# One 64 KB-row tile in place of tiles seven and eight of a contrast kernel on one core

## The chip, the core and the metric

The kernel runs on one core of a Trainium2 chip. A core has engines that work side by side, each through its own list of instructions in order: TensorE (PE in the profile, its weight loads PEld), VectorE (DVE), ScalarE (ACT), GpSimd (POOL) and SyncE (SP). Sixteen DMA engines carry data between the chip's large memory (HBM) and the core's working memory of 128 partitions (SBUF). A DMA is issued by one of the engines' sequencers; here SP issues all loads and ACT all stores. The metric is device microseconds (us) of one execution, and less is better.

## The reference

```
batch, c, h, w = 16, 3, 512, 512
x = random float32 in [0, 1);  factor = 1.5

mean = np.mean(x, axis=(2, 3), keepdims=True)
return np.clip(mean + factor * (x - mean), 0, 1)
```

There are 48 images of 512x512 float32 numbers, 50.33 MB in all. Each image needs its own mean before any of its pixels can be written. With that mean, a pixel becomes 1.5 x + (1 - 1.5) mean, cut to the range 0 to 1. So all 50.33 MB go in, and 50.33 MB come out.

## The kernel before

**Tiles.** A tile is four images: 128 partitions of 8192 numbers (`ROW`), 32 KB in each partition and 4.19 MB in all. An image fills 32 partitions. There are 12 tiles, counted from 0, so the seventh and the eighth are t = 6 and t = 7. In HBM a tile is one contiguous block, partition after partition.

**The ring.** SBUF holds one array `ring` of six slots (`BUFS`), one tile each; tile t lies in slot t % 6. Everything is done in place: a tile is loaded into its slot, summed there, overwritten with its result there, and stored from there. Tile t + 6 can be loaded only when the store of tile t has landed. The tile framework adds those waits; SP stands at each load until the slot is free.

**What is done with a tile.** `add` (lines 87 to 100) sums the 8192 numbers of every partition on ACT (line 96, a copy onto itself with an accumulator); tile 0 alone has part of its row summed on DVE (line 91). A matmul with a constant 128x128 matrix `blockw` (line 100) then sums the 32 partitions of each image, scales by (1 - factor) / pixels, and gives every partition its shift in a column of the PSUM array `bias`. `blockw` is made once by POOL (lines 62 to 72). `clip` (lines 102 to 114) runs two passes on DVE: factor times x plus shift (line 104), then max with 0 and min with 1 (line 112). `store` (line 85) is a DMA issued by ACT.

**The order.** The order is written out by hand (`tc.manual_schedule()`, lines 116 to 135), and each engine follows it. SP issues loads 0, 1, then tiles 2 and 3 with one DMA, tiles 4 and 5 with one DMA, then one DMA for each of the tiles 6 to 11. Tile 0 is clipped and stored in three pieces of 1024, 2048 and 5120 columns. From then on the loop clips tile t, sums tile t + 1 and stores tile t; for t = 1 and 3 the store is issued ahead of the sum, for the others behind it. As ACT both sums and issues stores, a store waiting on ACT holds up the sum behind it, and the other way about.

**The queues.** The profile calls the queue of the loads q1 and that of the stores q10. Each of the 16 DMA engines serves eight partitions of every transfer. A DMA moves one contiguous run as one packet, so a load of one tile is eight packets of 32 KB on each of the engines, and a load of two tiles is sixteen of them, the two tiles' rows in turn.

Of the kernel before, what the change touches and what calls it, by code (L numbers as in the profile page):

```python
# [1 line left out]

# [4 lines left out]


P = 128  # L10
ROW = 8192
BUFS = 6
FIRST = (1024, 3072)


@with_exitstack
def kernel(
    ctx: ExitStack,
    tc: tile.TileContext,
    x: bass.AP,  # L20
    factor: float,
    out: bass.AP,
):

    nc = tc.nc
    f32 = mybir.dt.float32
    Alu = mybir.AluOpType
    Act = mybir.ActivationFunctionType  # L30

    B, C, H, W = x.shape
    n_img, n_pix = B * C, H * W
    ppi = n_pix // ROW
    per_tile = P // ppi
    n_tiles = n_img // per_tile
    assert ppi * ROW == n_pix and per_tile * n_tiles == n_img

    factor = float(factor)
    wconst = (1.0 - factor) / float(n_pix)  # L40

    x_f = x.rearrange("b c h w -> (b c h w)")
    out_f = out.rearrange("b c h w -> (b c h w)")

    def dram(ap, t, c0=0, c1=ROW, n=1):
        run = [[P * ROW, n]] if n > 1 else []
        return bass.AP(
            tensor=ap.tensor, offset=t * P * ROW + c0, ap=[[ROW, P], *run, [1, c1 - c0]]
        )

    consts = ctx.enter_context(tc.tile_pool(name="consts", bufs=1))
    xpool = ctx.enter_context(tc.tile_pool(name="xpool", bufs=1))
    small = ctx.enter_context(tc.tile_pool(name="small", bufs=1))
    psum = ctx.enter_context(tc.tile_pool(name="psum", bufs=1, space=bass.MemoryType.PSUM))


    sums = small.tile([P, 2 * n_tiles], f32, name="sums")
    bias = psum.tile([P, n_tiles], f32, name="bias")

    blockw = consts.tile([P, P], f32, name="blockw")  # L60
    blocks = blockw.rearrange("p (a b) -> p a b", b=ppi)
    nc.gpsimd.memset(blockw, wconst)  # L62
    for base, step in ((0, -ppi), (ppi - 1, ppi)):
        nc.gpsimd.affine_select(  # L64
            out=blocks,
            in_=blocks,
            compare_op=Alu.is_ge,
            fill=0.0,
            base=base,
            pattern=[[step, per_tile], [0, ppi]],  # L70
            channel_multiplier=1 if step < 0 else -1,
        )


    ring = xpool.tile([P, BUFS, ROW], f32, name="ring")

    def slots(t, n=1, c0=0, c1=ROW):
        k = t % BUFS
        return ring[:, k, c0:c1] if n == 1 else ring[:, k : k + n, :]

    def load(t, n=1):
        nc.sync.dma_start(out=slots(t, n), in_=dram(x_f, t, n=n))  # L82

    def store(t, c0=0, c1=ROW):
        nc.scalar.dma_start(out=dram(out_f, t, c0, c1), in_=slots(t, 1, c0, c1))  # L85

    def add(t, c0=0):
        own = sums[:, 2 * t : 2 * t + 2]
        parts = []
        if c0:  # L90
            nc.vector.tensor_reduce(  # L91
                out=own[:, 0:1], in_=slots(t, 1, 0, c0), axis=mybir.AxisListType.X, op=Alu.add
            )
            parts.append(own[:, 0:1])
        part = slots(t, 1, c0)
        nc.scalar.activation(out=part, in_=part, func=Act.Copy, accum_out=own[:, 1:2])  # L96
        parts.insert(0, own[:, 1:2])
        shift = bias[:, t : t + 1]
        for k, part in enumerate(parts):
            nc.tensor.matmul(shift, blockw, part, start=k == 0, stop=k == len(parts) - 1)  # L100

    def clip(t, c0=0, c1=ROW):
        part = slots(t, 1, c0, c1)
        nc.vector.tensor_scalar(  # L104
            out=part,
            in0=part,
            scalar1=factor,
            scalar2=bias[:, t : t + 1],
            op0=Alu.mult,
            op1=Alu.add,  # L110
        )
        nc.vector.tensor_scalar(  # L112
            out=part, in0=part, scalar1=0.0, scalar2=1.0, op0=Alu.max, op1=Alu.min
        )

    with tc.manual_schedule():
        load(0)
        load(1)
        load(2, 2)
        load(4, 2)  # L120
        add(0, 4352)
        for c0, c1 in zip((0, *FIRST), (*FIRST, ROW)):
            clip(0, c0, c1)
            store(0, c0, c1)
        add(1)
        for t in range(1, n_tiles):
            clip(t)
            if t in (1, 3):
                store(t)
            if t + 1 < n_tiles:  # L130
                add(t + 1)
            if t not in (1, 3):
                store(t)
            if t + BUFS - 1 < n_tiles:
                load(t + BUFS - 1)


# [1 line left out]
_INS = ['x', 'factor']  # L139
_OUTS = [((16, 3, 512, 512), 'float32')]  # L140

_NUMBERS = {'factor': 1.5}


# [26 lines left out]
```

## Time and profile before

| What | Before |
|---|---|
| time, median of three runs | 239.47 us (239.06 to 239.49) |
| time of the profiled execution | 238.72 us |
| span of the profiled execution, first to last instruction | 237.0 us |
| busy in the span: PE / DVE / ACT / POOL | 7.6 / 112.1 / 82.9 / 1.0 us |
| one 128x8192 pass: ACT sum, DVE line 104, DVE line 112 | 7.03, 4.49, 4.43 us |
| bytes moved | 100.66 MB, half in, half out |

The profile is of one execution. Its span runs from the first to the last instruction; the 1.72 us between the span and that execution's time lie outside it. An engine's busy time leaves out the time in which its sequencer waits or issues DMAs. The slices of the profile's second part are a fortieth of the span, 5.9 us each.

### The profile page before, as it was taken

Reading aid. Unit: us, or ns where it says so; the run is one execution under the profiler, and the core shown is the slowest. Engines: PE = TensorE matmul, PEld = TensorE weight load, DVE = VectorE, ACT = ScalarE, POOL = GpSimd, SP = SyncE. Lnnn points to the kernel's source line nnn. Section 1 sums busy time; section 2 is a strip of 40 time slices with the busy share of each in tenths; the row PEclk is TensorE's granted clock in tenths of the full one; section 3 lists DMA queues with packets and bytes.
Section 4 is the critical chain, followed back from the end, with each engine's and each line's share of the span. In section 5 each row is a group of like instructions: output and inputs, shape, how many; then the busy total and the mean of one; then the engine's idle time right before and its main releaser. Section 6 shows DMA issues by size and latency. Waiting matters only on the chain.

```text
span 237.0 us, 211 instructions
## 1 busy us (share of the span) xinstructions
PE 7.6 (3%) x26; PEld 6.5 (3%) x26; DVE 112.1 (47%) x29; ACT 82.9 (35%) x25; POOL 1.0 (0%) x7
## 2 busy tenths in 40 slices
PE   0000000000000000000000000000000000000000
PEld 0000000000000000000000000000000000000000
DVE  0078708609990059979209407704902920950000
ACT  2050190299100894650380091083056029000000
POOL 1000000000000000000000000000000000000000
DMA  7999998999999999999999999999999999999996
GB/s 265 442 442 442 398 459 383 441 428 435 465 426 404 409 442 442 442 442 442 442 426 431 404 420 442 442 442 442 442 442 426 415 398 442 442 442 442 442 442 265
DMA packets 3712, 100.66 MB, mean 425 GB/s; under 512 B 384, under 2 KB 384, under 8 KB 512
## 3 DMA queue, kind: packets, MB, share of 16 engines
q1 hardware_dynamic: 1696, 50.33, 49.6%
q10 hardware_dynamic: 2016, 50.33, 49.2%
HBM read 50.33 MB, written 50.33 MB: 425 GB/s over the span
## 4 chain that ended last, share of the span: by engine, by line
DMA 39%; DVE 25%; another core or an unknown queue 11%; ACT 9%; issue 3%; PE 1%; ACTq 1%; SPq 0%
DMA out_dram<-ring 20%; DMA ring<-in_x_dram 18%; DVE ring L104 11%; DVE ring L112 11%; ACT ring L96 9%; DVE sums L91 2%; PE bias L100 1%; ACTq L85 1%; SPq L82 0%
## 5 line engine op out<-in xcount | busy, mean ns | idle before, releaser
L96 ACT ACTIVATE ring<-ring 128x8192 f32<-128x8192 f32 (+1 forms) x12 | 80.7, 6724 | 117.3 <-DMA ring<-in_x_dram 95.3
L104 DVE TENSOR_SCALAR ring<-ring,bias 128x8192 f32<-128x8192 f32 (+3 forms) x14 | 54.3, 3880 | 84.9 <-PE bias L100 84.9
L112 DVE TENSOR_SCALAR ring<-ring 128x8192 f32<-128x8192 f32 (+3 forms) x14 | 53.4, 3817 | 0.5
L100 PE MATMUL bias<-sums,blockw 128*128 128x1 f32 x26 | 7.6, 361 | 194.0 <-ACT ring L96 193.5
L100 PEld LDWEIGHTS bias<-sums,blockw 128*128 128x128 f32 x26 | 6.5, 312 | 195.0 <-ACT ring L96 177.7
L91 DVE TENSOR_REDUCE sums<-ring 128x1 f32<-128x4352 f32 x1 | 4.7, 4685 | 13.1 <-DMA ring<-in_x_dram 13.1
L96 ACT ACTIVATION_READ_ACCUMULATOR ring<-ring 128x1 f32 x12 | 2.2, 186 | 0.0
L96 ACT ACT_TABLE_LOAD x1 | 1.3, 1283 | 0.8 <-PEq L152 0.8
L64 POOL TENSOR_SCALAR_AFFINE_SELECT blockw<-blockw 128x128 f32<-128x128 f32 x2 | 0.6, 311 | 0.1
L62 POOL MEMSET blockw<- 128x128 f32 x1 | 0.2, 204 | 0.3 <-POOLq L152 0.3
L152 POOL MEMSET const-uint8-127<- 128x1 uint8 x1 | 0.1, 103 | 0.0
L152 POOL MEMSET const-bfloat16-1.0<- 128x1 bf16 x1 | 0.1, 102 | 0.0
L152 POOL MEMSET const-float32-0.0<- 128x1 f32 x1 | 0.1, 98 | 0.3 <-issue 0.3
L152 POOL MEMSET const-float32-1.0<- 128x1 f32 x1 | 0.1, 98 | 0.0
## 6 DMA issues: line engine op xcount, KB each, us to landing
out_dram<-ring ACTq DMA_DIRECT2D x11, 4096.0 KB, 48.5
ring<-in_x_dram SPq DMA_DIRECT2D x8, 4096.0 KB, 31.4
ring<-in_x_dram SPq DMA_DIRECT2D x2, 8192.0 KB, 59.5
out_dram<-ring ACTq DMA_DIRECT2D x1, 2560.0 KB, 37.3
out_dram<-ring ACTq DMA_DIRECT2D x1, 1024.0 KB, 25.8
out_dram<-ring ACTq DMA_DIRECT2D x1, 512.0 KB, 16.1
```

Of the source, the lines that this page charges most:

```text
L62: nc.gpsimd.memset(blockw, wconst)
L64: nc.gpsimd.affine_select(out=blocks, in_=blocks, compare_op=Alu.is_ge, fill=0.0, base=base, pattern=[[step, per_tile], [0, ppi]], channel ...
L85: nc.scalar.dma_start(out=dram(out_f, t, c0, c1), in_=slots(t, 1, c0, c1))
L91: nc.vector.tensor_reduce(out=own[:, 0:1], in_=slots(t, 1, 0, c0), axis=mybir.AxisListType.X, op=Alu.add)
L96: nc.scalar.activation(out=part, in_=part, func=Act.Copy, accum_out=own[:, 1:2])
L100: nc.tensor.matmul(shift, blockw, part, start=k == 0, stop=k == len(parts) - 1)
L104: nc.vector.tensor_scalar(out=part, in0=part, scalar1=factor, scalar2=bias[:, t : t + 1], op0=Alu.mult, op1=Alu.add,)
L112: nc.vector.tensor_scalar(out=part, in0=part, scalar1=0.0, scalar2=1.0, op0=Alu.max, op1=Alu.min)
L152: nc = _bacc.Bacc("TRN2", target_bir_lowering=False, num_devices=1)
```

## The change

- The constant `PAIR = (6, 7)` names two tiles that are treated as one tile of 128 rows of 16384 numbers (64 KB). The pair holds the same eight images; now an image fills 16 of the 128 rows. Slots 0 and 1 of the ring lie side by side in a partition, so a row of the pair is contiguous in SBUF as well as in HBM.
- It is loaded by two DMAs as before, but each now brings half of the columns: a run of 32 KB out of every 64 KB of HBM, into slot 0 and then into slot 1.
- Both halves are summed on ACT one after the other. Their matmuls use a second constant matrix, `widew`, with blocks of 16 rows, and gather in one column of `bias`: the matmul of the first half opens the sum, that of the second half closes it. Both halves are clipped after that.
- It is stored by one DMA of 8.39 MB with rows of 64 KB, issued behind the stores of t = 8 and t = 9 (the ninth and tenth tile) and ahead of those of 10 and 11.
- From t = 8 on, each tile is summed, clipped and stored in turn, so the store is issued ahead of the next tile's sum.
- Tiles 2 and 3 are loaded with a DMA each.

```
+PAIR = (6, 7)
...
     def dram(ap, t, c0=0, c1=ROW, n=1):
+        if t in PAIR:
+            wide, half = 2 * ROW, t - PAIR[0]
+            return bass.AP(
+                tensor=ap.tensor,
+                offset=PAIR[0] * P * ROW + half * ROW,
+                ap=[[wide, P], [1, n * ROW]],
+            )
...
+    def block_weights(name, rows):
+        w = consts.tile([P, P], f32, name=name)
+        blocks = w.rearrange("p (a b) -> p a b", b=rows)
+        nc.gpsimd.memset(w, wconst)
+        for base, step in ((0, -rows), (rows - 1, rows)):
+            nc.gpsimd.affine_select(
...
+    blockw = block_weights("blockw", ppi)
+    widew = block_weights("widew", ppi // 2)
...
+    def store_pair():
+        nc.scalar.dma_start(out=dram(out_f, PAIR[0], n=2), in_=slots(PAIR[0], 2))
...
-        shift = bias[:, t : t + 1]
+        if t in PAIR:
+            shift, w, start, stop = PAIR[0], widew, t == PAIR[0], t == PAIR[1]
+        else:
+            shift, w, start, stop = t, blockw, True, True
+        shift = bias[:, shift : shift + 1]
         for k, part in enumerate(parts):
-            nc.tensor.matmul(shift, blockw, part, start=k == 0, stop=k == len(parts) - 1)
+            nc.tensor.matmul(
+                shift, w, part, start=start and k == 0, stop=stop and k == len(parts) - 1
+            )
...
         load(0)
         load(1)
-        load(2, 2)
+        load(2)
+        load(3)
         load(4, 2)
...
-        for t in range(1, n_tiles):
+        for t in range(1, BUFS):
             clip(t)
             if t in (1, 3):
                 store(t)
-            if t + 1 < n_tiles:
+            if t + 1 < BUFS:
                 add(t + 1)
             if t not in (1, 3):
                 store(t)
-            if t + BUFS - 1 < n_tiles:
-                load(t + BUFS - 1)
+            load(t + BUFS - 1)
+        load(2 * BUFS - 1)
+        add(PAIR[0])
+        add(PAIR[1])
+        for t in PAIR:
+            clip(t)
+        for t in (8, 9):
+            add(t)
+            clip(t)
+            store(t)
+        store_pair()
+        for t in (10, 11):
+            add(t)
+            clip(t)
+            store(t)
```

## The prediction

> **What bounds the kernel now.** I read the page's second and third part first (are the DMA engines ever idle?), then its table of DMA issues.
>
> ```profile
> DMA  7999998999999999999999999999999999999996
> GB/s 265 442 442 442 398 459 383 441 428 435 465 426 404 409 442 442 442 442 442 442 426 431 404 420 442 442 442 442 442 442 426 415 398 442 442 442 442 442 442 265
> ...
> q1 hardware_dynamic: 1696, 50.33, 49.6%
> q10 hardware_dynamic: 2016, 50.33, 49.2%
> ```
>
> The two queues together fill 49.6 + 49.2 = 98.8% of sixteen engines' span; only the first and the last slice are not full. VectorE at 47% and ScalarE at 35% are far from it. The second view is busy time by stretches; the last two columns of a row are the DMA share and GB/s.
>
> ```profile
> 3.00:20.00 17.00, 1.15 (x4) 1.00 (x4) 6.17 (x4) 3.50 (x2) 0.00 (x0) 1.00 1.00 430
> ...
> 116.42:135.77 19.35, 0.59 (x2) 0.50 (x2) 8.92 (x2) 7.12 (x2) 0.00 (x0) 1.00 1.00 434
> ...
> 193.87:235.80 41.93, 0.58 (x2) 0.50 (x2) 8.92 (x2) 7.12 (x2) 0.00 (x0) 1.00 0.98 425
> ```
>
> The first row has loads alone, the second loads and stores in equal parts, the third stores alone. The rate is the same in all three, so neither direction nor their mixture is the limit: the engines themselves are. The trace's records of single packets say the same: the median 32 KB packet takes 1.213 us, for load and store alike, and one of 20 KB 0.761, of 8 KB 0.309, of 4 KB 0.159.
>
> That gives a budget. 100.66 MB are 192 packets of 32 KB on each engine, 192 x 1.213 = 232.9 us. The first packet starts at 1.81 and the last ends at 235.83, so the engines have 234.0 us for it: 1.1 us is lost, 0.65 of it in the first packet of each engine (mean 1.87 us in place of 1.213), most of the rest in loads between 35 and 54 us, some of which take 1.31 to 1.52 us. The other 3.0 us of the span are the start (1.81) and the end behind the last packet (1.18).
>
> Third, the order of time around the change, in the timeline: start, length, engine.
>
> ```profile
> 103.35 0.34 ACTq L85 DMA_DIRECT2D out_dram<-ring  x1
> ...
> 116.42 7.03 ACT L96 ACTIVATE ring<-ring 128x8192 f32<-128x8192 f32 x1 [12.25 <-DMA ring<-in_x_dram]
> ...
> 135.77 7.03 ACT L96 ACTIVATE ring<-ring 128x8192 f32<-128x8192 f32 x1 [12.23 <-DMA ring<-in_x_dram]
> ...
> 155.14 7.03 ACT L96 ACTIVATE ring<-ring 128x8192 f32<-128x8192 f32 x1 [12.25 <-DMA ring<-in_x_dram]
> ```
>
> The first row issues the store of tile 5; the others sum tiles 7, 8 and 9, each as its load lands, and further down tile 10 follows at 174.50, tile 11 at 193.87. By the landings' semaphores the store of tile 5 lands at 162.32, those of 6 to 11 at 181.72, 197.48, 207.17, 216.86, 226.52 and 236.18. The last store is issued at 210.65 and waits until 226.5 for those ahead of it. So the end is the store queue's length, not any computation.
>
> **The change part by part.**
>
> *Does the store queue run dry?* This decides, because stores 6 and 7 leave the place behind store 5. Loads wait only for the landings of stores 0 to 5, which keep their order and their time, so loads 6 to 11 land as before (97.02, 116.39, 135.75, 155.12, 174.47, 193.84). ACT: store 5 at 103.35, sum of 6 from 103.7 to 110.8 (it was 97.05; load 7 lands later, so nobody waits), sum of 7 at 116.42, its matmul done at 124.2 (row: sum 7.03 + read 0.19 + matmul 0.6). DVE then runs four passes, 124.2 + 2 x (4.49 + 4.43) + gaps = 142.1. Sum of 8 at 135.77, shift at 143.5, clip to 152.5, store 8 issued at 152.5. Store 5 holds the queue until 162.3: 9.8 us to spare. Store 9: load 155.12, sum, matmul and clip take 16.7, issued at 171.9, against the end of store 8 at 181.7 (the time of the old store 6: both share with loads 10 and 11). The pair is issued at 172.3, against 197.5. Store 10 at 174.5 + 16.7 = 191.2, against 216.9. Store 11 at 210.6, against 226.5. Every store is in the queue 9.8 us or more before its turn. Cost 0.
>
> *Waits that ACT now takes.* Store 8 waits on ACT for its clip until 152.5, and behind it stands the sum of 9, whose data land at 155.12; store 10 waits until 191.2, and the sum of 11 behind it starts at 193.84. 2.6 us to spare in both; and if a sum came later, the 9.8 us and 15.9 us above would still cover it. Cost 0.
>
> *The store of 64 KB rows.* From the packets of 20 and 32 KB: (1.213 - 0.761) / 12288 bytes = 36.8 ps a byte, so 0.008 us of a packet doesn't grow with its size. Eight packets of 64 KB in place of sixteen of 32 KB save 8 x 0.008 = 0.06 us. No row shows a packet over 32 KB. Low end: -0.06. High end: the slowest store packet seen is 1.220, 0.007 over the median, on sixteen: +0.1. I take -0.06, the line through four sizes.
>
> *Loads of half rows.* The same 16 packets of 32 KB per engine, but the rows that an engine reads one after the other lie 64 KB apart, and its neighbours' twice as far away as before. Low end 0: in the trace the engines already work at starts that are multiples of 32 KB apart, at 1.213. High ends by slower rows: the mean load packet between 20 and 50 us, 1.2275, would cost 16 x 0.0145 = 0.23; the edge of the slow group, 1.312, 16 x 0.099 = 1.6; the slowest, 1.522, 4.9. I take 0, as the runs stay 32 KB long and a load of two tiles, whose successive packets lie 4.19 MB apart, already ran near the full rate (430 GB/s from 36 to 54 us).
> A rule speaks against it: the Trainium skill, "DMA: Bandwidth & Descriptors", section "Latency and other measured facts", says that rows in HBM a large power of two apart slow copies, from a pitch of 512 KiB at full rate (207 GB/s per direction) to 164 at 2 MiB. By its figures 64 KB would be free, and the sum would stay; if its slope began as low as here, it would be the second case below.
>
> *Loads 2 and 3 apart.* One more issue on SP, 0.43 us by its neighbours, at 2.1 us, when the queue has 9.7 us of work and more; the next load isn't needed before 45. Tile 2 lands at about 34 (half of the stretch 22.77 to 45.27) in place of 45. Nothing starts sooner: its sum stands on ACT behind store 1, which waits for a clip until 45.33. Ends: 0, and -0.31, if all that the 337 load packets between 20 and 50 us lose (337 x 0.0145 / 16) came from alternating rows; I take 0, since the slow ones stand where the small store pieces of tile 0 land (35, 48, 65 us), and those remain.
>
> *The rest.* POOL makes `widew`: 0.20 + 2 x 0.31 = 0.8 us behind 1.76; first needed at about 111. Matmuls are as many. Both cost 0 under the 100 us that cover them.
>
> Sum: -0.06. The profiled execution's span goes from 237.0 to 236.9, its time from 238.72 to 238.66. The median of the runs is 0.75 above the profiled one, so 239.47 - 0.06 = 239.4.
> By the skill's same page (section "Where 436 GB/s comes from") a core's DMA ports carry at most 435.2 GB/s; by that 100.66 MB need at least 231.3 us, so no packing could win more than 1.6 of the 232.9 us. The trace's 433 in steady stretches agrees with such a ceiling.
>
> **The rivals.**
>
> *Half-row loads are slow (slower).* Place: loads 6 and 7, 78 to 117 us. Price 1.6 at 1.312 us a packet: 241.0; it decides from 1.243 us a packet (16 x 0.030 = 0.48). For it: loads are the only packets that vary at all (1.31 to 1.52 around 35 to 54). Against it: 960 later ones average 1.2156, with every kind of address.
>
> *A wait on a store's issue (slower).* If an issue behind the pair waits for the pair's landing (the program has few DMA semaphores, and they are used again), the queue runs dry at 216.9: 1.01 from issue to first packet (0.80 to 1.81) and 0.4 of spread between the sixteen landings, 1.4 in all: 240.9. Against it: no store of before shows such a wait, and at the pair's issue only loads 10 and 11 and stores 8 and 9 are under way.
>
> *The queue runs dry at 162 (slower).* Late stores alone cost nothing at first: loads 10 and 11 then have 15.8 us of work left at the full rate (6.1 of load 10 and 9.7 of load 11) and take the engines meanwhile. So it decides from 9.8 + 15.8 = 25.6 us beyond the 152.5 worked out for store 8; past that each us costs one. At 26.6 us late, 240.4. Against it: the rows that it is worked out from are steady to 0.02 us.
>
> *Early loads lose less (faster).* Both gains in full, -0.06 - 0.31 = -0.37: 239.1. To pass 0.2% it would need all of the 0.45 us lost after the first packets and the 0.06 as well, 239.0.
>
> *The pair's store is cut to 32 KB packets.* Then nothing is saved: 239.5.
>
> **How the numbers follow.** I hold 0.2% (0.48 us) to be about what a measurement of this kernel tells from no change; the three runs spread 0.43. Forecast 239.4, with the uncut and the cut pair: 0.65. Slow half rows: 0.15. A wait on an issue: 0.05. A dry queue: 0.02. Faster: 0.13, which also holds what the profiled execution may not show, since the runs are 0.75 above it. Slower by over 0.2% is 0.15 + 0.05 + 0.02 = 0.22. The likeliest case alone has 239.0 to 239.9. The range for 8 in 10 goes down to 238.9, past the faster case of 239.0, and up to 241.0, the slow half rows at 1.312; what is over that (packets slower still, two waits) I give 1 in 10.
>
> **What would show it.** Right: the DMA share by stretches stays 1.00 at 433 GB/s from 97 to 194 us, loads 6 and 7 take 19.4 us each as before, the pair lands at about 217 with packets near 2.42 us, and the last store at 236.1. Wrong: a stretch below 0.95 (dry queue, or a wait that the chain names), load packets of 6 and 7 over 1.24 us, pair packets over 2.48 us. The weakest points are the two things that no row shows: 64 KB packets and the 64 KB pitch.

## The result and the profile after

The changed kernel takes 240.41 us (median of 22 runs, 238.85 to 241.39) against 239.06 us before (22 runs, 238.73 to 239.49): a ratio of 1.0049, 95% interval 1.0036 to 1.0063. By that ratio it is slower by about 1.2 us; the medians lie 1.35 apart. The forecast was no change: 239.4 if one starts from the first three runs of the kernel before, as it did (239.47), and 239.0 from all 22. The 22 runs of the changed kernel are not one heap: three lie at 238.9 to 239.0, where the kernel before lies, the other nineteen at 239.8 to 241.4. All runs were at the full granted clock; in two experiments below the runs of one kernel spread by more than 1.5%, so that most of them may be in a slow state, and there the fastest run is given beside the median. The profiled execution took 240.46 us with a span of 238.7.

The page of the changed kernel, the lines on DMA:

```profile
DMA  7999999999999999999999999999999999898994
GB/s 264 439 439 434 401 460 395 419 425 428 463 434 423 428 417 434 434 434 423 439 434 439 439 439 439 439 439 412 434 417 434 434 439 500 362 516 357 439 439 181
...
q1 hardware_dynamic: 1712, 50.33, 49.5%
q10 hardware_dynamic: 1872, 50.33, 48.9%
```

The engines are as full as before until the last slice, which moves 181 GB/s in place of 265. (The 362 and 357 stand beside 500 and 516: a packet is counted whole where it starts, and the pair's packets of 64 KB take 2.418 us each.) The store queue has 144 packets fewer: 128 are the halved count of the pair's store, 16 the end packets of the store that is saved. The load queue has 16 more, the end packets of one more load. Two stretches of busy time look different; the last two columns are the DMA share and GB/s:

```profile
36.00:54.00 18.00, 1.14 (x4) 0.96 (x4) 9.16 (x3) 8.04 (x3) 0.00 (x0) 1.00 0.97 399
...
236.00:237.60 1.60, 0.00 (x0) 0.00 (x0) 0.00 (x0) 0.00 (x0) 0.00 (x0) 1.00 0.05 20
```

From 36 to 54 us the rate is 399 GB/s, against 430 before. The next stretch, 54 to 78 us, goes the other way. Before, and then the changed kernel:

```profile
36.00:54.00 18.00, 0.91 (x4) 0.74 (x4) 9.39 (x3) 8.27 (x3) 0.00 (x0) 1.00 1.02 430
54.00:78.00 24.00, 0.59 (x2) 0.50 (x2) 17.28 (x4) 6.17 (x3) 0.00 (x0) 1.00 0.98 421
```

```profile
54.00:78.00 24.00, 0.58 (x2) 0.50 (x2) 17.50 (x4) 6.10 (x2) 0.00 (x0) 1.00 1.02 439
```

Over both stretches that is about 425 GB/s before and 422 now, so most of the dip to 399 is only a matter of where packets start. The end of the kernel is another thing. There are 1.6 us with a DMA share of 0.05 and 20 GB/s. One engine of sixteen is a share of 0.06: a single DMA engine is still at work when the other fifteen have finished. The end packets of the last store say it too: the middle one of the sixteen lands at 236.31, the fifteenth at 236.47, the last at 237.92. Before, the middle one was at 235.93 and the last at 236.18. Every sum starts later, too (timeline; sums of tiles 8 to 11):

```profile
139.43 7.03 ACT L112 ACTIVATE ring<-ring 128x8192 f32<-128x8192 f32 x1 [12.71 <-DMA ring<-in_x_dram]
...
158.92 7.03 ACT L112 ACTIVATE ring<-ring 128x8192 f32<-128x8192 f32 x1 [12.37 <-DMA ring<-in_x_dram]
...
178.50 7.03 ACT L112 ACTIVATE ring<-ring 128x8192 f32<-128x8192 f32 x1 [12.46 <-DMA ring<-in_x_dram]
...
198.05 7.03 ACT L112 ACTIVATE ring<-ring 128x8192 f32<-128x8192 f32 x1 [12.42 <-DMA ring<-in_x_dram]
```

Before they started at 135.77, 155.14, 174.50 and 193.87. Two things add up in this. By its semaphore the load of tile 8 is complete on fifteen engines at 137.29 (135.68 before): the loads as a whole trail by 1.6 us. The late engine brings it at 139.41, another 2.1 us. Its gap to the fifteenth grows from 1.3 us at the load of tiles 4 and 5 (79.20 and 80.50) to 2.6 us at tile 11 (195.39 and 198.03). No store comes late from it; those that the change moves are issued at 156.22, 175.70 and 176.07:

```profile
156.22 0.34 ACTq L98 DMA_DIRECT2D out_dram<-ring  x1
...
175.70 0.34 ACTq L98 DMA_DIRECT2D out_dram<-ring  x1
176.07 1.26 ACTq L101 DMA_DIRECT2D out_dram<-ring  x1
```

The stores ahead of them land at 161.46, 180.91 and 199.26, so each is in the queue in time.

The late engine is behind from early on: load 3 lands on fifteen engines by 45.58 and on the last at 46.27. Soon after that stand slow load packets: of those that start from 46 to 53 us, 22 took over 1.3 us, on average 1.62 and up to 1.97; before it was 18, on average 1.41, up to 1.52. They catch the eye, but they are not what sets the late engine apart. When the packets are put in order engine by engine (how is shown below), the late engine loses 0.33 us on slow packets from 46 to 54 us and the others 0.31 to 0.91. From 78 to 195 us, though, the late engine loses 1.36 us, nearly all of it in loads, and the fifteen others nothing (0.00).

All this begins more than a hundred microseconds ahead of the pair's store, and the engine is behind ahead of the first half-row load. The only part of the change that has happened by then, besides POOL's second matrix, is the separate loading of tiles 2 and 3.

### The profile page after: what moved, and what is told of

It reads as the page before. It is cut to its first block, busy times and chain, and to the rows that moved or that the text cites. A ratio compares the mean times of both kernels' runs of the same rounds, so it can differ in the third digit from the quotient of the medians.

```text
span 238.7 us, 213 instructions
## 1 busy us (share of the span) xinstructions
PE 7.5 (3%) x26; PEld 6.5 (3%) x26; DVE 112.0 (47%) x29; ACT 82.9 (35%) x25; POOL 1.7 (1%) x10
## 4 chain that ended last, share of the span: by engine, by line
DMA 39%; DVE 25%; another core or an unknown queue 12%; ACT 6%; issue 6%; PE 1%; ACTq 0%; SPq 0%
DMA ring<-in_x_dram 21%; DMA out_dram<-ring 19%; DVE ring L130 11%; DVE ring L138 11%; ACT ring L112 6%; DVE sums L107 2%; PE bias L120 1%; ACTq L98 0%; SPq L95 0%
## 5 line engine op out<-in xcount | busy, mean ns | idle before, releaser
L120 PE MATMUL bias<-sums,blockw 128*128 128x1 f32 x22 | 6.4, 360 | 167.3 <-ACT ring L112 166.8
L120 PEld LDWEIGHTS bias<-sums,blockw 128*128 128x128 f32 x22 | 5.5, 310 | 168.2 <-ACT ring L112 150.6
L120 PE MATMUL bias<-sums,widew 128*128 128x1 f32 x4 | 1.1, 355 | 30.9 <-ACT ring L112 30.9
L120 PEld LDWEIGHTS bias<-sums,widew 128*128 128x128 f32 x4 | 1.0, 310 | 31.1 <-issue 18.6
L73 POOL TENSOR_SCALAR_AFFINE_SELECT widew<-widew 128x128 f32<-128x128 f32 x2 | 0.7, 343 | 0.0
```

What stands on the lines that cost most here:

```text
L73: nc.gpsimd.affine_select(out=blocks, in_=blocks, compare_op=Alu.is_ge, fill=0.0, base=base, pattern=[[step, P // rows], [0, rows]], chann ...
L120: nc.tensor.matmul(shift, w, part, start=start and k == 0, stop=stop and k == len(parts) - 1)
```

## Experiments: which part of the change

The four kernels of this section ran beside 29 runs of the kernel before (239.0 us).

**Loads 2 and 3 apart, alone** (kernel before):

```
-        load(2, 2)
+        load(2)
+        load(3)
```

> The kernel before with one edit: tiles 2 and 3 are loaded by a DMA each. In the profile of the changed kernel one DMA engine is late in the load queue from about 46 us on, and its slow load packets (up to 1.97 us) stand between 43 and 51 us, long before the pair is touched. Theory 1 (the early loads: without the alternating rows of two tiles the engines meet slow reads there): this alone gives about 240.3, with one engine landing 1 us or more behind the other fifteen. Theory 2 (the half rows 64 KB apart slow the reads): within 0.3 of before, 239.1, no late engine. Theory 3 (the later order or the 64 KB store): within 0.3 of before.

Measured 239.96 us, ratio 1.0033 (1.0018 to 1.0049), 12 runs from 238.83 to 240.74. So most of the loss comes with this edit alone, and with the same scatter. (The intervals of this ratio and of the changed kernel's overlap, so a further part of the loss is not shown.) The profiled execution happened to be one of the good ones, 239.10 us, and it has no late engine (the last end packet 0.22 us behind the middle one), although its slow packets are there (up to 2.0 us).

**The changed kernel with loads 2 and 3 in one again:**

```
-        load(2)
-        load(3)
+        load(2, 2)
```

> The changed kernel with tiles 2 and 3 loaded by one DMA again, as before. Theory 1 (early loads): back to 239.1, and the slow packets around 43 to 51 us fall back from 1.4 to 1.9 us to at most 1.5. Theories 2 and 3 (half rows; order or 64 KB store): 240.3 as the changed kernel.

Measured 239.01 us, ratio 1.0001 (0.9993 to 1.0010). All else of the change, the half rows, `widew`, the new order and the pair's store, costs nothing that can be measured, and gains nothing. One detail of the expectation was not met: the longest load packet was 1.64 us, not at most 1.5.

**Half-row loads alone** (kernel before; loads 6 and 7 at a pitch of 64 KB):

```
+        if t in (6, 7):
+            src = bass.AP(
+                tensor=x_f.tensor,
+                offset=6 * P * ROW + (t - 6) * ROW,
+                ap=[[2 * ROW, P], [1, ROW]],
+            )
```

> The kernel before with one edit: loads 6 and 7 bring the column halves of 64 KB rows, stores and order as before. (It leaves the sums and the places of the stored rows of those two tiles as they were, so those eight images come out wrong; the traffic is what counts.) Theory 2 (half rows): 240 or more, with load packets over 1.213 us between 78 and 117 us. Theories 1 and 3: 239.1.

Measured 239.03 us, ratio 1.0001 (0.9992 to 1.0009). The stretches of loads 6 and 7 run at the full rate:

```profile
78.00:97.05 19.05, 1.17 (x4) 1.00 (x4) 9.94 (x3) 14.13 (x4) 0.00 (x0) 1.00 1.02 440
97.05:116.42 19.37, 0.59 (x2) 0.50 (x2) 16.72 (x4) 7.12 (x2) 0.00 (x0) 1.00 1.00 431
```

This falls as a cause. It agrees with the Trainium skill, "DMA: Bandwidth & Descriptors", section "Latency and other measured facts", whose figures for slow copies begin at a pitch of 512 KiB, far above 64 KB.

**The new order with plain tiles** (changed kernel, tiles 6 and 7 as whole rows with a shift each, one joint store of 32 KB packets):

```
+PLAIN = True
...
-        if t in PAIR:
+        if t in PAIR and not PLAIN:
...
-        col = PAIR[0] if t in PAIR else t
+        col = PAIR[0] if t in PAIR and not PLAIN else t
```

> The changed kernel with tiles 6 and 7 as two plain tiles again (whole rows of 32 KB loaded, each its own shift), still stored by one DMA behind the stores of 8 and 9, now in packets of 32 KB; the order of all work and the separate loads of 2 and 3 stay. Theory 1 (early loads): 240.3 as the changed kernel. Theory 2 (half rows) and the part of theory 3 that is the 64 KB packet: 239.1. The part of theory 3 that is the order: 240.3.

Measured 240.37 us, ratio 1.0060 (1.0047 to 1.0073): slow without any 64 KB row, because loads 2 and 3 are apart.

## Experiments: why separate loads are slower

The next four asked whether the kind of rows matters. They ran beside 17 runs of the kernel before (239.0 us).

**Tiles 2 to 5 with a DMA each** (kernel before):

```
-        load(2, 2)
-        load(4, 2)
+        load(2)
+        load(3)
+        load(4)
+        load(5)
```

> The kernel before with tiles 2, 3, 4 and 5 loaded by a DMA each. With only 2 and 3 apart the time was 239.96, the slow load packets (up to 2.0 us) stood at 46 to 53 us, just when the load of tiles 4 and 5 in turn begins. Theory A (the step from single rows to the rows of two tiles in turn makes them): no slow packets at 46 to 53 us, 239.0. Theory S (the small store packets of tile 0 beside single-tile reads make them): as slow as with 2 and 3 apart, about 240, slow packets still there.

Measured 252.04 us (six runs, 242.75 to 254.39); even the fastest is 3.8 us over the kernel before. Neither theory had that. The page of the profiled execution, 254.39 us:

```profile
DMA  7999999999999999999999999999999999986900
GB/s 285 456 420 426 430 432 415 393 472 420 415 420 472 425 410 410 410 462 451 410 410 415 431 446 436 394 425 446 399 420 446 425 425 436 451 368 265 415 26 21
```

The last two slices move 26 and 21 GB/s, the rate of one engine (433 / 16 = 27): fifteen engines end at 240.9, one at 251.7. It is the late engine again, in this execution grown large.

**Tiles 4 and 5 with a DMA each, 2 and 3 in one** (kernel before):

```
-        load(4, 2)
+        load(4)
+        load(5)
```

> The kernel before with tiles 4 and 5 loaded by a DMA each; 2 and 3 stay in one. Theory A (a step between the two kinds of load at 45 us, here the other way round): 239.5 to 240. Theory S (what counts is the kind of read beside the small stores, which last until 65 us): slow packets over 1.6 us from 45 to 65 us and about 239.5 or more. If only the rows of 2 and 3 matter: 239.0.

Measured 240.39 us, ratio 1.0054 (1.0034 to 1.0074). That is a little over theory A's 239.5 to 240. Theory S is met here (239.5 or more, slow packets over 1.6 us: up to 1.78). But in the run above theory A had 239.0 and theory S about 240, and both were far off.

**Tile 0 stored by one DMA,** with loads 2 and 3 apart, and in the kernel before:

```
             clip(0, c0, c1)
-            store(0, c0, c1)
+        store(0)
```

> Tiles 2 and 3 by a DMA each as in the run that gave 239.96, and tile 0 stored by one DMA of 32 KB rows behind its last piece, so that no store packet of 4, 8 or 20 KB is left. Theory S: the slow load packets between 43 and 53 us are gone (loss of all loads from 20 to 54 us under 0.1 us a DMA engine in place of 0.70), no late engine, 238.6 to 239.0. Theory A: the loss and the late engine stay, 239.9.

> The kernel before with tile 0 stored by one DMA of 32 KB rows behind its last piece; loads as before. Theory S: the 0.43 us that loads lose from 20 to 54 us goes, 238.6, faster by 0.4. Theory A: 239.0, or slower if the small early stores serve something that the profile doesn't show (the store queue starts at 28 in place of 20 us).

Measured 242.51 (ratio 1.0144, 1.0130 to 1.0158) and 242.20 us (1.0137, 1.0118 to 1.0155). One sign of theory S came true: without the small store packets no load packet from 46 to 53 us takes over 1.3 us. Yet both kernels are slower, by 3.2 us in the kernel before, whose loads are untouched. The loss has moved: 1.7 to 1.8 us an engine from 97 to 194 us, where the kernel before loses nothing. So theory S falls, and with it the idea that the slow packets at 46 us make the time. (The edit also moves the first store from 20 to 28 us.) So neither theory stood, and there had to be something that both the number of loads and the number of stores change.

**What the packets show.** The trace has every DMA packet with its queue, size and start. Chained end to start they give one DMA engine's list (two engines whose packets end within 4 ns of each other can be mixed up in it); L is a load, S a store, the number its KB, and a star the 4-byte end packet that tells the semaphore. First the kernel before, then the changed one:

```
31.36 L32  32.57 S4   32.73 L32                       33.94 S4   34.09 L32  35.30 S*   35.31 L32  36.60 S8
31.46 L32  32.67 S4   32.83 L*   32.83 S4   32.99 L32  34.20 S*   34.20 L32  35.41 S8
```

The two queues take turns, packet by packet. The Trainium skill says so as well ("DMA: Bandwidth & Descriptors", section "Queues, rings and completion order"), and the trace agrees. What I had missed is that the end packet takes a turn too. The separate load of tile 2 ends at 32.83 with a star, and in that turn the load queue moves 4 bytes where it would have moved 32 KB. The store queue gets the next turn, so the stores are one packet ahead, and nothing brings that back: from then on each store has its end packet and so has each load. Later in the same two executions:

```
115.81 L*  115.82 S32  117.03 L32 ...  121.87 L32  123.08 S*
117.40 L*  117.40 S32  118.61 L32 ...  121.03 L32  122.24 S*
```

From the end of a load to the end of the store beside it were 7.27 us, three load packets and three store packets; now it is 4.84 us, two and two. I call lead the number of packets (mean over the engines) of the load under way that had started when the store of tile 3 ended; by the moment at which one counts it moves by up to 0.2. A DMA more in the load queue while tile 0 is being stored takes 1 off the lead, a DMA more in the store queue adds 1. (With tile 0 stored at once and 2 and 3 apart, load 2 has ended on most engines when the store begins, so its end packet does not count.) This puts the runs into three groups, at about 3.4, at 2.1 to 2.4 and below; within a group it does not order the times:

| Kernel | Lead | Last end packet behind the middle, us | Median, us |
|---|---|---|---|
| before | 3.5 | 0.25 | 239.06 |
| changed, 2 and 3 in one load | 3.4 | 0.40 | 239.01 |
| half rows alone | 3.4 | 0.67 | 239.03 |
| changed | 2.4 | 1.61 | 240.41 |
| 2 and 3 apart | 2.4 | 0.22 | 239.96 |
| plain tiles, new order | 2.2 | 1.69 | 240.37 |
| 4 and 5 apart | 2.1 | 2.50 | 240.39 |
| 2 and 3 apart, tile 0 stored at once | 1.3 | 2.41 | 242.51 |
| before, tile 0 stored at once | 1.5 | 1.95 | 242.20 |
| 2 to 5 apart | 1.2 | 10.89 | 252.04 |

Leads and end packets are from the one profiled execution of each, the medians from all its runs. For 2 and 3 apart that execution was a good one.

## Experiments: moving the lead

Theory T is that the lead decides. It forecasts that changes without any bearing on the rows read make a kernel fast or slow. The first four ran beside 18 runs of the kernel before (239.1 us).

**The changed kernel with one end packet more in the store queue** (the last piece of tile 0 stored in two halves of the partitions):

```
+            for p in (0, P // 2):
+                nc.scalar.dma_start(
+                    out=bass.AP(tensor=out_f.tensor, offset=p * ROW + c0,
+                        ap=[[ROW, P // 2], [1, c1 - c0]]),
+                    in_=ring[p : p + P // 2, 0, c0:c1],
+                )
```

> The changed kernel with one edit: the last piece of tile 0 (5120 columns) is stored by two DMAs of 64 partitions each in place of one of 128; bytes and packets are the same. In the traces every DMA ends with a 4-byte packet on each engine that takes a turn of its queue, so the other queue gets a turn more. Separate loads of tiles 2 and 3 add one such turn to the load queue, and from then on the loads trail: whenever a store of a tile ends, an engine has started 2.4 packets (mean) of the load under way, against 3.4 before. Theory T (this lead of the loads is what decides): one end packet more in the store queue brings the lead back to 3.4 and the time to 239.0. Theory A (it is the kind of row order read at 45 us): 240.4 as the changed kernel.

Measured 240.62 us, ratio 1.0056 (1.0034 to 1.0078). The lead was 3.3 as meant, and from 97 to 194 us the packets lost next to nothing (0.02 us an engine). But store packets of the halved piece took up to 2.23 us in place of 0.761, the two queues' packets lost 0.9 us an engine between 36 and 78 us, and the last engine ended 2.1 us behind. Engine by engine, the two that end last lost 2.2 and 2.3 us from 54 to 78 us, on packets of the halved piece, and 0.1 or less after that. So the run does not meet theory T's forecast, but what it loses is in large part the price of the halves.

**Loads 2 and 3 in one, but in two halves of the partitions** (kernel before):

```
-        load(2, 2)
+        for p in (0, P // 2):
+            nc.sync.dma_start(
+                out=ring[p : p + P // 2, 2:4, :],
+                in_=bass.AP(tensor=x_f.tensor, offset=2 * P * ROW + p * ROW,
+                    ap=[[ROW, P // 2], [P * ROW, 2], [1, ROW]]),
+            )
```

> The kernel before with one edit: tiles 2 and 3 are loaded by two DMAs of 64 partitions each, the rows of the two tiles in turn as before, so that only an end packet comes into the load queue. Theory T: lead 2.4, time 239.9 to 240.4 as with a DMA for each tile. Theory A (the order in which rows are read): 239.0.

Measured 257.00 us, ratio 1.0757 (1.0733 to 1.0781), far from both. The page shows why it tells nothing on the lead:

```profile
GB/s 303 431 416 329 211 246 241 241 236 298 433 434 431 431 442 421 431 442 436 421 442 426 442 431 431 442 421 431 442 436 421 447 426 436 431 436 431 426 431 267
```

While the halves are loaded (about 22 to 60 us) the rate falls to 211 to 246 GB/s, and their packets take 1.9 to 2.6 us: these loads of 64 partitions are slow in themselves.

**Tiles 2 to 5 apart, with two end packets more in the store queue** (the second and third piece of tile 0 in halves, as above):

> The kernel in which tiles 2 to 5 have a DMA each (252.0, lead 1.3), with the second and the third piece of tile 0 stored by two DMAs of 64 partitions each: two end packets more in the store queue. Theory T: lead 3.4, time 239.0. Theory A: stays at 250 or so.

Measured 239.95 us, ratio 1.0034 (1.0020 to 1.0048), against 252.04 without them (242.75 at the fastest). The lead is 3.3 and the far-off engine is gone (0.98 us behind in place of 10.9). The loads and the rows are those of the run at 252; with two halved stores even the slowest run, 240.32, is 2.4 us under the fastest without them. It did not go all the way to 239.0. Slow load packets of up to 1.81 us at 46 us and the price of the halves may be why; this was not tested.

**The kernel before with one end packet more in the store queue** (third piece in halves):

> The kernel before with the last piece of tile 0 stored by two DMAs of 64 partitions: lead 4.4, which no run so far has. Theory T, if a longer lead is better still or no worse: 238.7 to 239.0; if 3.4 is the best lead, slower. Theory A: 239.0.

Measured 239.47 us, ratio 1.0016 (1.0006 to 1.0027), lead 4.4. Here too store packets of the halved piece were slow (up to 1.24 us for 20 KB), so it could not say whether the lead or the halves cost the 0.4 us.

The last set moves the lead without halves (28 runs of the kernel before, 239.05 us).

**The changed kernel with tiles 3, 4 and 5 in one load:**

```
         load(2)
-        load(3)
-        load(4, 2)
+        load(3, 3)
...
-            if t in (1, 3):
+            if t in (1, 2, 3):
```

(and `not in (1, 2, 3)` further down.)

> The changed kernel with tiles 3, 4 and 5 in one load, their rows in turn, behind a load of tile 2 alone (and the store of tile 2 issued ahead of the next sum, since tile 3 now lands at about 77 us). Tile 2 stays apart, but the load queue has one end packet less than in the changed kernel while tile 0 is stored. Theory T (the lead of the loads decides): lead 3.4 and 239.0. Theory A (the kind of row order at the step from one to several tiles): slow packets at 46 us and 240 or more.

Measured 239.25 us, ratio 1.0006 (0.9997 to 1.0016), lead 3.4, last engine 0.18 us behind. Tile 2 is still loaded alone, and the kernel is as fast as before within the measurement. The slow load packets from 46 to 53 us are all there: 17 over 1.3 us, on average 1.72 and up to 1.85, slower than the changed kernel's on average. Here they cost next to nothing.

**The kernel before with a tiny load:**

```
+    spare = small.tile([16, 128], f32, name="spare")
...
         load(2, 2)
+        nc.sync.dma_start(out=spare, in_=bass.AP(tensor=x_f.tensor, offset=0, ap=[[ROW, 16], [1, 128]]))
         load(4, 2)
```

> The kernel before with one load more, of 16 rows of 512 bytes that nobody uses, between the loads of tiles 2 and 3 and of 4 and 5: on each engine one packet of 512 bytes and an end packet, two turns of the load queue, some 0.03 us of work. Theory T: lead 1.4, and 242 or more, as in the other runs with that lead. Theory A: 239.1.

Measured 249.79 us (243.12 to 250.01; five of six runs at 249.8 to 250.0). 8 KB that nobody reads cost 4.1 us in the fastest run and 10.7 at the median. In the profiled execution, 243.12 us, the lead is 1.1 by data packets, about as meant; theory T had "242 or more" and nothing that would tell 243 from 250.

**The changed kernel with the first store 1.2 us later:**

```
-FIRST = (1024, 3072)
+FIRST = (2176, 4224)
```

> The changed kernel with tile 0 clipped and stored in pieces of 2176, 2048 and 3968 columns in place of 1024, 2048 and 5120: the first store is issued 1.2 us later, which is one load packet. No DMA is added or taken away, no load changed. Theory T: lead 3.4, 239.0 to 239.3. Theory A: 240.4.

Measured 239.02 us, ratio 0.9999 (0.9990 to 1.0007), against 240.41 with the pieces as they were. Not a DMA is added, taken away or changed in its rows; only the sizes of tile 0's three pieces and so the moment of the first store. The first store packets start at 25.7 us on most engines in place of 24.5. The lead is 3.2, and the last engine lands 0.33 us behind the middle one. The stretch that was at 399 GB/s (where packets start counts here too):

```profile
36.00:54.00 18.00, 0.90 (x4) 0.72 (x4) 9.40 (x3) 8.28 (x3) 0.00 (x0) 1.00 0.99 420
```

**The kernel before with the same pieces:**

> The kernel before with the pieces of 2176, 2048 and 3968 columns. Theory T: lead 4.4; the run with that lead and a store in two halves gave 239.47, with 0.4 us lost to the halves, so 239.0 to 239.2 here, or slower if 3.4 is a best value. Theory A: 239.0.

Measured 239.01 us, ratio 0.9997 (0.9988 to 1.0006), lead 4.4. A longer lead is no better.

**Two more profiles,** of the changed kernel and of the one with the tiny load:

> The changed kernel once more, for a second profile. If a late engine is what makes its time, then the time of this execution above 239.0 is, to 0.3 us, the time by which the last DMA engine's end packet of the last store lands behind the middle of the sixteen (1.6 us in the profile of 240.46, 0.3 us in a profile of 239.10 with the separate loads alone).

> The kernel with the tiny load once more, since the profiled execution took 243.12 and the others about 249.8. If late engines make the time: at about 249.8 one engine lands 8 us or more behind the others at the end, with slow packets on that engine alone. If instead all packets are slower at 249.8, the sixteen land within 2 us and the mean packet is over 1.24 us.

The changed kernel took 240.49 us, 1.49 above 239.0, and its last end packet lands 1.71 us behind the middle one: as expected. Its stretches:

```profile
36.00:54.00 18.00, 0.80 (x3) 0.63 (x3) 9.49 (x3) 8.38 (x3) 0.00 (x0) 1.00 0.98 402
236.00:237.70 1.70, 0.00 (x0) 0.00 (x0) 0.00 (x0) 0.00 (x0) 0.00 (x0) 1.00 0.05 19
```

The tiny load's kernel took 242.34 us this time, with the middle engine at 237.25 and the last at 239.70, so here all engines are late, and some of them later than the others. No execution of 249.8 was profiled, and the question on it stays open.

**Engine by engine.** The lead is a mean, and it hides what single engines do. In the lists of packets one can count, for each engine and each load of a tile between 75 and 200 us, how many of the load's packets had started when the store beside it ended. (Loads whose list cannot be told from another engine's are left out.) All twenty profiled executions together:

| Load packets started at the store's end | Loads counted | Time over the usual packet times in one, mean, us | Most |
|---|---|---|---|
| 0 | 30 | 0.98 | 4.52 |
| 1 | 414 | 0.25 | 1.19 |
| 2 | 521 | 0.003 | 0.46 |
| 3 or more | 698 | 0.001 | 0.10 |

An engine that is two packets or more into the load loses nothing; one that is a single packet in loses a quarter of a microsecond with a tile, on average. In the kernel before all sixteen engines stand at 3. One end packet more in the load queue moves them to 2, where nothing is lost yet, but an engine that was one short goes to 1. In the profile of the changed kernel there is one such engine, and it is the late one. Its first packet of all took 2.40 us, the longest of the sixteen; its first store packet came behind 17 load packets, on the others behind 18 or 19. So it is one short before it loses anything by it. In the second profile there are two engines with 17, and they are the two that end last. In the good execution with 2 and 3 apart all engines have 18 and then 2, and none is late. With tiles 2 to 5 apart fifteen engines are at 1, and the one that began with 17 is at 0: it is the one that ends 10.9 us behind.

## Why the prediction was wrong

**What bounds the kernel** was right, and so was the budget of packets: a 32 KB packet still takes 1.213 us, and the changed kernel's loss is not more work but one engine that ends 1.6 us after the others.

**The step that failed** is the term "Loads 2 and 3 apart", put at 0 between a gain of 0.31 and 0. It looked at when the issue comes, when tile 2 lands and who waits for it, and all of that held (tile 2 landed at 33.97, its sum waited for the issue of store 1). It did not ask what one DMA more does to the order in which the engines serve the two queues, and it named no loss as possible and gave no reason to exclude one. Alone it costs 0.33% (239.96), and without it the rest of the change is at 1.0001. What the runs showed in its place: the end packet of the additional load costs the load queue a turn, the loads run one packet closer behind the stores, and an engine that is only one packet into a load when a store ends loses 0.25 us with a tile, on average.

**The early loads.** The only rival on them, "Early loads lose less", went the wrong way: from 20 to 54 us they lose 0.77 us an engine in place of 0.43. But this is not the loss that counts, as they lose 0.74 in the run at 239.01. That the long load packets stand where the small stores of tile 0 land was borne out by the runs that store tile 0 at once.

**The store queue** stayed full, with the issues about 4 us later than worked out (156.2 for 152.5, 175.7 for 171.9, 195.3 for 191.2), because the loads land later on all engines, and later still on the late one; the spare time covered it. The worked landings of the loads, "as before", were off by that: load 8 at 139.41, not 135.75.

**The 64 KB packets** took 2.418 us, exactly the line through the four smaller sizes. The gain of 0.06 us is too small to be seen in 1.0001.

**The half rows** cost nothing, as taken (1.0001); the rival that made them slow was wrong. The median of 240.41 lies close to that rival's 241.0, and inside the range for 8 in 10, which went up to 241.0 for that rival's sake; this is luck, as it is not its mechanism.

**The wait on an issue and the dry queue** did not come. POOL's matrix and the matmuls cost nothing, as the run at 1.0001 includes them.

**What is shown and what is not.** Shown: the loss comes with the separate loads; it comes back to nothing when the first store is delayed by one packet, with the separate loads still there, and when another load is merged; it appears in the kernel before when the loads gain a DMA or the stores lose some. In the profiles, the loads from 75 us on that lose time are nearly all on engines at 0 or 1 of the table above; in the changed kernel the late engine is short before it loses anything by it. This is read from the packets, and fits the edits that move the count. It also fits the scatter: at a mean lead of 2.4 it depends on the execution how many engines come out one short, and at 1.1 to 1.5 nearly all are at 1 or 0. Not shown: why a load that is one packet in when a store ends meets slower packets, what makes the slow packets at 46 to 53 us, and why the tiny load's kernel takes 249.8 us in most runs and 242 to 243 in the two profiled ones. The run with the halved third store in the changed kernel does not fit theory T without the price of halves, which was read from its packets (2.2 and 2.3 us on two engines) but not tested apart.

## What to carry to other kernels

When two DMA queues keep the engines full, splitting or merging a transfer need not be free even if bytes, data packets and waits stay the same. Here it shifted the two queues against each other for the rest of the kernel. So look at the packets engine by engine, not only at a rate or a mean over the engines, and at when the last of the sixteen lands. If a harmless edit of that kind costs a fraction of a per cent, moving the first transfer of the other queue by one packet time is a cheap way to test it, and here it also mended it. None of the kernels beat the one before, whose engines spend 232.9 of 237.0 us on packets at their usual rate.

## What the runs showed of the hardware that was not expected

- The 4-byte packet that ends a DMA takes a turn of its queue on each engine; it lasts 9 ns, and the other queue then gets a packet of 32 KB ahead of its time.
- With load and store queue both full, an engine that was one packet of 32 KB into a load when the store beside it ended lost 0.25 us with a tile on average (414 loads), one that was two in 0.003 us (521 loads).
- A tiny load of 16 rows of 512 bytes, put between two large ones, took a kernel from 239.05 us to 243.12 in its fastest run of six and 249.79 at the median.
- Loads of 64 partitions in place of 128, with 16 packets of 32 KB an engine as before, ran at 211 to 246 GB/s in place of some 430, with packets of 1.9 to 2.6 us.
- One engine alone can fall 10.9 us behind its fifteen neighbours, all with the same bytes to move (the kernel with tiles 2 to 5 apart, in an execution of 254.39 us).
- The issue of the 8.39 MB store with rows of 64 KB took ACT's sequencer 1.26 us (0.98 in another run), against 0.34 for a store of one tile. Nothing waited for it here.
